# Second layer's input projection: the second 1024 weight rows in seven products too, beside attention

## The chip, the cores and the metric

The kernel runs on one core of one Trainium2 chip. The metric is the device time of one execution in microseconds (us).

## The reference, cut to what matters

Two sequences (512 and 256 tokens, 768 together, width 2048) go through two layers. The change lies in the second one:

```python
h = x @ odd_w_in[i]                       # [768, 2048] @ [2048, 8192]
q, k, v, g = jnp.split(h, 4, axis=-1)     # 16 heads of 128 each
y = (_dilated_mixture(q, k, v, pos) * jax.nn.silu(g)) @ odd_w_out[i]
x = _layernorm(DN_ALPHA * x + y, ln_g[layer], ln_b[layer])
```

`_dilated_mixture` turns the first 32 of each head's 128 features of q and k by position (rope), and is then attention within each sequence, with a fixed table added to the scores. Everything is float32. A product is made of three float32r matmuls: each factor is split in a high part (a cast, on ACT) and a low part (what is left, a subtraction on DVE or POOL), and high by high, high by low and low by high are summed.

## The kernel before

Activations lie feature-major: `xh` and `xl` hold 16 tiles of 128 features by 768 tokens. The projection of the second layer goes in two passes over the 2048 weight rows (the contraction).

**First pass, rows 0 to 1023** (class `Seven`, L664 to L778). Two blocks of 128 output features at a time (a *pair*, 32 pairs) are computed by Strassen's scheme: the weights of a pair are four tiles of 512 rows by 128 columns, the activations four quarters (512 features by 384 tokens), and seven products of 12 matmuls (128x384) take the place of eight. Sums and differences of the activation quarters are made once; those of the weights in `prep` (four subtractions and seven splits a pair, DVE L708 and L442, ACT L441); the sums of products in `product` (five additions out of PSUM on DVE, L738, and two copies on ACT, L740 and L742). `prep` is called three products ahead (`AHEAD = 3`), and the split weights have four buffers. The partial sums of each pair go to DRAM (`pd1`). `run` calls `each()` after every product, which takes one item off the list `c.q` of side work.

At the end of the pass the plain activations of rows 1024 to 2047 are restored from `z` by eight splits.

**Second pass, rows 1024 to 2047**, head by head for 16 heads: four blocks (q, k, v, gate), each of 48 matmuls 128x384 (`proj_f` with `k0=8`, L521), after which DVE adds the partial sum that was loaded from `pd1` some blocks before (`block`, L1293). q and k get rope on 32 partitions by 768 tokens and are split (`qk`, L1307 to L1310 and L442: shuffle, products with cos and sin, sum, cast on ACT, low part on POOL). Attention (class `Attn`) goes in steps of 128 queries, six steps a head: `scores`, two steps later `turn` (the probabilities transposed and split), three steps later `values` once a sequence is done. In `scores` DVE scales, adds the table and takes the maximum, negates it, ACT takes the exponential, DVE the reciprocal of the sum and the scaling of the probabilities (L827 to L832). The steps of a head are put into `c.q`, and run between the matmuls of later blocks:

```python
hd.qq = qk(block(h, 0), h % 2 * 2)
hd.kk = qk(block(h, 1), h % 2 * 2 + 1)
flush(c)
att.add(hd)
c.q += [nop] * (2 if h < 15 else 1) + [att.step] * (6 if h < 15 else att.left())
```

The output projection (`proj_t`, L565) follows; its activations are the heads' results, loaded back from `md` (`mix_in`) and split.

**What sets the order.** Each engine works off its queue in order and waits where an operand is late. The order in a queue is not simply that of the code: the framework plans the queues before the run, by its own expectation of durations, code order being the priority. DMAs are issued from SP, ACT or POOL; the issuing queue waits for the data that the DMA reads.

Of the kernel before, what the change touches and what calls it, by code (L numbers as in the profile page):

```python
# [665 lines left out]
class Seven:  # L666
# [11 lines left out]
    def __init__(self, c, ops, cols, dst, pool, outs):  # L678


        self.c, self.ops, self.cols, self.dst, self.pool, self.outs = c, ops, cols, dst, pool, outs
        self.raw, self.hl, self.acc, self.res = {}, {}, {}, {}

    def rows(self, n, b):
        w, f0, f1 = self.cols[n]
        return wf(w, b // 2, (f0, f1)[b % 2])
# [16 lines left out]
    def prep(self, n, i):  # L703
# [5 lines left out]
        new = lambda: self.pool.tile([128, 512], F32, tag="bt", name="bt", bufs=4)  # L709
# [12 lines left out]
    def product(self, n, i):  # L722
# [6 lines left out]
        xh, xl = self.ops[i]  # L729
# [35 lines left out]
    def run(self, seq, each):  # L765

        at = {}
        for m, (n, i) in enumerate(seq):
            at.setdefault(n, m)
        due = sorted(at.items(), key=lambda x: x[1])  # L770
        for m in range(-self.AHEAD, len(seq)):
            while due and due[0][1] <= m + self.AHEAD + 5:
                self.load(due.pop(0)[0])
            if m + self.AHEAD < len(seq):
                self.prep(*seq[m + self.AHEAD])
            if m >= 0:
                self.product(*seq[m])
                each()  # L778


class Attn:
# [5 lines left out]
    def __init__(self, c, pool, table=None, early=None):  # L787
        self.c, self.pool, self.table, self.early = c, pool, table, early or pool
        self.units, self.n = [], 0
# [9 lines left out]
    def step(self):  # L799
        u, n = self.units, self.n  # L800
        if n < len(u):
            self.scores(*u[n])
        if 0 <= n - 2 < len(u):
            self.turn(*u[n - 2])
        if 0 <= n - 3 < len(u) and u[n - 3][1] == u[n - 3][0].nt - 1:
            self.values(u[n - 3][0])
# [5 lines left out]
    def scores(self, seq, i):  # L812
# [13 lines left out]
        else:  # L826
            nc.vector.tensor_tensor_reduce(out=p, in0=s, in1=self.table[:, 384 - 128 * i:384 - 128 * i + nk],  # L827
                                           scale=1.0 / SQ128, scalar=-3e38, op0=ALU.add, op1=ALU.max, accum_out=st[:, 0:1])
# [3 lines left out]
        nc.vector.tensor_scalar(out=p, in0=p, scalar1=st[:, 2:3], scalar2=0.5, op0=ALU.mult, op1=ALU.mult)  # L832
# [4 lines left out]
    def turn(self, seq, i):  # L837
        c, nc, pool = self.c, self.c.nc, self.pool
        nt = seq.nt
        if i == 0:  # L840
            seq.pt = [pool.tile([128, nt, 128 * nt], F32R, tag=f"pt{x}{nt}", name=f"pt{x}{nt}") for x in "hl"]
# [4 lines left out]
        split_ps(nc, pv, *(t[:, :, 128 * i:128 * i + 128] for t in seq.pt))  # L846

    def values(self, seq):
        c, nc = self.c, self.c.nc
        nt = seq.nt  # L850
        o = ps_tile(c, "ps_o")[:, 0:128 * nt]
# [5 lines left out]
        seq.head.done(o, seq.t0, nt)  # L857
# [25 lines left out]
def hybrid_kernel(tc, x_p, x_s, w_in0, w_out0, a_re, a_im, log_dt, b_re, b_im, c_re, c_im, d_sk, glu_w, glu_b,  # L883
# [4 lines left out]
    with ExitStack() as es:  # L888
# [22 lines left out]
        pd1 = dr.tile([32, 128, 2, TOK], F32, name="pd1")  # L911
# [127 lines left out]
        with rpool("pk") as pk, ExitStack() as bes:  # L1039
# [89 lines left out]
            for k in range(8):  # L1129
# [5 lines left out]
        cols1 = ([(w1, 128 * h, 2048 + 128 * h) for h in range(16)] +  # L1135
                 [(w1, x + 256 * j, x + 256 * j + 128) for x in (4096, 6144) for j in range(8)])
        with rpool("po") as po:
# [90 lines left out]
            ops = half(0, 0), half(0, 3), half(8, 0), half(4, 0), half(8, 3), half(12, 0), half(4, 3)  # L1228
            n_first = 3
            with rpool("pw") as pw:  # L1230
                free, whole = [z[:, t, 0:768] for t in range(6)], {}

                def outs(n):
                    two = lambda f: [f[:, 0:HALF], f[:, HALF:768]]
                    if n < n_first:
                        return [pw.tile([128, HALF], F32, tag="early", name="early", bufs=2 * n_first) for _ in range(2)]
                    whole[n] = free.pop(0), free.pop(0)
                    free.extend(whole[n])
                    return two(whole[n][0]) + two(whole[n][1])

                def part_out(n, r):
                    if n < n_first:
                        for i in range(4):
                            store(c, pd1[n, :, i // 2, HALF * (i % 2):HALF * (i % 2) + HALF], r[i], 1)
                    else:
                        for i in range(2):
                            store(c, pd1[n, :, i], whole[n][i], 1)

                sv = Seven(c, ops, cols1, part_out, pw, outs)
# [10 lines left out]
                sv.run(sv.order(0, 32, n_first), lambda: fill(c))  # L1260
                flush(c)
                for k0, t0 in ((8, 0), (12, 3), (8, 3), (12, 0)):
                    for k in range(k0, k0 + 4, 2):
                        hi, lo = (a[:, k:k + 2, 128 * t0:128 * t0 + HALF].rearrange("p k (t n) -> p t k n", t=3) for a in (xh, xl))
                        raw = z[:, t0:t0 + 3, 128 * k:128 * k + 256].rearrange("p t (k n) -> p t k n", k=2)
                        split_sb(nc, raw, hi, lo, nc.vector)

        res0 = pool("res0", 1).tile([128, 6, 256], F32, name="res0")
# [9 lines left out]
        with rpool("pc") as pc:  # L1278
            cos1 = pc.tile([32, TOK], F32, name="cos1")
            sin1 = pc.tile([32, TOK], F32, name="sin1")  # L1280
            nc.sync.dma_start(cos1, c_rope1[0])
            nc.sync.dma_start(sin1, c_rope1[1])
            mixt = pc.tile([128, 896], F32, name="mixt")
            nc.sync.dma_start(mixt, c_mix)
            att = Attn(c, pc, mixt)

            def block(n, i):

                w, *f = cols1[n]
                t = raws.pop(0)  # L1290
# [3 lines left out]
                return t  # L1294

            raws, plan = [], []

            def fetch():

                if plan:  # L1300
                    n, i = plan.pop(0)
                    raws.append(pc.tile([128, TOK], F32, tag="raw", name="raw", bufs=4))
                    nc.sync.dma_start(raws[-1], pd1[n, :, i])

            def qk(t, k):
                sh = pc.tile([32, TOK], F32, tag="sh", name="sh", bufs=1)
                nc.vector.stream_shuffle(sh, t[0:32], SWAP)  # L1307
# [4 lines left out]
                return c.xh[k], c.xl[k]  # L1312

            def turn_v(t, i):

                vv = [a[4 + i].rearrange("p (t f) -> p t f", t=6) for a in (c.xh, c.xl)]

                def go():
                    for t0, n in SEQS:
                        ps = ps_tile(c, "ps_v")  # L1320
                        for j in range(n):
                            nc.tensor.transpose(ps[:, 128 * j:128 * j + 128], t[:, 128 * (t0 + j):128 * (t0 + j) + 128], c.ident)
                        split_ps(nc, ps[:, 0:128 * n].rearrange("p (j f) -> p j f", j=n), *(a[:, t0:t0 + n] for a in vv))

                return vv, go
# [5 lines left out]
            def mix_in(k):  # L1331
                if k < 15:
                    load_split(pc, md[k], c.xh[k], c.xl[k], 4, nc.vector, "raw")

            class Head1:
                def __init__(self, h):
                    self.h = h
# [7 lines left out]
                def v(self, t):  # L1345
                    return [a[:, t] for a in self.vv]

                def done(self, o, t0, nt):
                    if t0 == 0:
                        self.o = pc.tile([128, TOK], F32, tag="o1", name="o1", bufs=2)  # L1350
                    nc.scalar.copy(self.o[:, 128 * t0:128 * (t0 + nt)], o)
                    if t0:
                        self.finish()

                def finish(self):
                    nc.gpsimd.tensor_tensor(out=self.o, in0=self.o, in1=self.g, op=ALU.mult)
                    if self.h < 15:
                        store(c, md[self.h], self.o, 0)
                    else:
                        split_sb(nc, self.o, c.xh[15], c.xl[15])  # L1360

            for h in range(16):
                plan += [(h, 0), (h, 1), (16 + h // 2, h % 2), (24 + h // 2, h % 2)]
            fetch()
            fetch()
            for h in range(16):
                hd = Head1(h)
                fetch()
                hd.qq = qk(block(h, 0), h % 2 * 2)
                fetch()  # L1370
                hd.kk = qk(block(h, 1), h % 2 * 2 + 1)
                flush(c)
                att.add(hd)
                c.q += [nop] * (2 if h < 15 else 1) + [att.step] * (6 if h < 15 else att.left())
                fetch()
                hd.vv, go = turn_v(block(16 + h // 2, h % 2), h % 2)
                c.q.insert(0, go)
                fetch()
# [126 lines left out]
```

## Time and profile before

| | |
|---|---|
| runs | 2730.73, 2731.81, 2734.80 us (median 2731.81) |
| profiled execution | 2731.15 us, span 2729.3 us |
| PE (matmul) busy | 2613.1 us, 96% of the span |
| DVE, ACT, POOL busy | 1775.7, 903.7, 798.0 us |
| mean granted TensorE clock | 0.982 |
| first pass | about 1254 to 1741 us |
| second pass with attention | about 1741 to 2431 us |

PE is pipelined: a matmul's own duration (334 ns) is about twice the distance between two starts. For rates one reads distances and windows, not means.

### The profile page before, as it was taken

How to read it: one execution, taken by the hardware profiler on the slowest of the kernel's cores; microseconds unless marked ns; L12 is line 12 of the kernel's file. 1: busy time of each engine (PE TensorE's matmuls, PEld its weight loads, DVE VectorE, ACT ScalarE, POOL GpSimd, SP SyncE). 2: the span in 40 equal slices, each digit the busy share in tenths (PEclk: the TensorE clock that was granted, in tenths of full speed). 3: DMA queues.
4: the chain of work that ended last, by engine and by line, in shares of the span. 5: the costliest groups of instructions: out<-in, count | busy, mean ns of one | idle time of the engine just before them, and what ended most of it. 6: DMA issues, size and time to landing. Idle time of an engine off the chain costs nothing.

```text
span 2729.3 us, 41667 instructions
## 1 busy us (share of the span) xinstructions
PE 2613.1 (96%) x15824; PEld 2493.2 (91%) x15824; DVE 1775.7 (65%) x3504; ACT 903.7 (33%) x1775; POOL 798.0 (29%) x554
## 2 busy tenths in 40 slices
PE   8899999998998999998999999999999999999997
PEld 7899999998997898887999999999999999998886
DVE  6578888858357842238766666577767677773527
ACT  4222222222235521116433333334333333341111
POOL 2645555536554430002000000222212122234404
PEclk9999999999999999998999999999999999999998
DMA  5333333332434362225344434333332333345222
GB/s 149 114 91 93 98 92 93 90 80 75 128 109 136 121 219 74 66 82 178 122 126 132 125 123 135 116 97 101 93 97 87 98 101 95 106 136 183 76 69 112
DMA packets 349769, 301.56 MB, mean 110 GB/s; under 512 B 57665, under 2 KB 298561, under 8 KB 348673
## 3 DMA queue, kind: packets, MB, share of 16 engines
q1 hardware_dynamic: 337712, 287.13, 34.5%
q0 software_dynamic: 2496, 8.39, 1.1%
q10 hardware_dynamic: 9360, 3.38, 0.8%
q8 instruction: 125, 2.05, 0.3%
q14 instruction: 76, 0.61, 0.1%
HBM read 231.38 MB, written 67.44 MB: 109 GB/s over the span
## 4 chain that ended last, share of the span: by engine, by line
PE 75%; DVE 12%; DMA 4%; issue 3%; POOL 2%; SPq 2%; ACT 2%; DVEq 0%; ACTq 0%; POOLq 0%
PE pt L565 22%; PE pa L521 13%; PE pb L521 13%; PE ps_y L733 7%; PE ps_z L733 5%; PE ps_x L733 5%; PE ps_o L856 3%; PE ps_sc L820 3%; PE ps_pt L844 2%; DVE tmpv L227 1%; DMA wr<-in_even_w_in_dram 1%; SPq L351 1%; PE ps_y L410 1%; DVE ca L229 1%; DVE win L229 1%
## 5 line engine op out<-in xcount | busy, mean ns | idle before, releaser
L441 ACT CAST wh<-wr 128x512 fp32r<-128x512 f32 x442 | 273.9, 623 | 895.9 <-PE pt L565 334.1
L442 DVE TENSOR_TENSOR wl<-wr,wh 128x512 fp32r<-128x512 f32 x274 | 241.4, 884 | 359.6 <-ACT wh L441 359.5
L565 PE MATMUL pt<-wh,xh 128*128 128x256 f32 (+1 forms) x1392 | 458.4, 330 | 7.8 <-ACT wh L441 6.8
L565 PE MATMUL pt<-wl,xh 128*128 128x256 f32 (+1 forms) x1392 | 457.0, 328 | 1.5 <-POOL wl L442 1.3
L565 PE MATMUL pt<-wh,xl 128*128 128x256 f32 (+1 forms) x1392 | 456.1, 328 | 0.0
L521 PE MATMUL pa<-xh,wh 128*128 128x384 f32 x960 | 337.7, 352 | 21.4 <-ACT wh L441 18.1
L442 POOL TENSOR_TENSOR wl<-wr,wh 128x512 fp32r<-128x512 f32 x168 | 232.9, 1397 | 354.9 <-ACT wh L441 313.0
L521 PE MATMUL pa<-xh,wl 128*128 128x384 f32 x960 | 326.3, 340 | 9.8 <-POOL wl L442 9.6
L521 PE MATMUL pa<-xl,wh 128*128 128x384 f32 x960 | 325.7, 339 | 0.0
L521 PE MATMUL pb<-xl,wh 128*128 128x384 f32 x960 | 325.3, 339 | 0.0
L521 PE MATMUL pb<-xh,wl 128*128 128x384 f32 x960 | 325.1, 339 | 0.0
L521 PE MATMUL pb<-xh,wh 128*128 128x384 f32 x960 | 325.0, 339 | 0.0
L565 PEld LDWEIGHTS pt<-wh,xh 128*128 128x128 f32 x1392 | 265.6, 191 | 32.6 <-ACT wh L441 7.7
L565 PEld LDWEIGHTS pt<-wl,xh 128*128 128x128 f32 x1392 | 266.2, 191 | 24.6 <-POOL wl L442 1.8
L565 PEld LDWEIGHTS pt<-wh,xl 128*128 128x128 f32 x1392 | 266.1, 191 | 22.4
L521 PEld LDWEIGHTS pa<-xh,wh 128*128 128x128 f32 x960 | 182.8, 191 | 26.1 <-ACT wh L441 20.2
L521 PEld LDWEIGHTS pa<-xh,wl 128*128 128x128 f32 x960 | 182.9, 191 | 13.1 <-POOL wl L442 13.1
L521 PEld LDWEIGHTS pb<-xh,wh 128*128 128x128 f32 x960 | 183.4, 191 | 1.5
L521 PEld LDWEIGHTS pa<-xl,wh 128*128 128x128 f32 x960 | 183.1, 191 | 0.0
L521 PEld LDWEIGHTS pb<-xl,wh 128*128 128x128 f32 x960 | 183.1, 191 | 0.0
L521 PEld LDWEIGHTS pb<-xh,wl 128*128 128x128 f32 x960 | 182.7, 190 | 0.0
L1275 POOL DMA_DIRECT2D lrow<-in_ln_g_dram x8 | 4.5, 563 | 477.8 <-DMA wr<-in_odd_w_in_dram 475.8
(350 smaller groups left out, 5569.6 us busy)
## 6 DMA issues: line engine op xcount, KB each, us to landing
wr<-in_even_w_in_dram SPq DMA_DIRECT2D x144, 256.0 KB, 3.2
wr<-in_odd_w_in_dram SPq DMA_DIRECT2D x134, 256.0 KB, 2.9
b<-in_odd_w_in_dram SPq DMA_DIRECT2D x128, 256.0 KB, 2.9
raw<-pd SPq DMA_DIRECT2D x64, 384.0 KB, 3.4
pd<-z SPq DMA_DIRECT2D x58, 384.0 KB, 2.5
wr<-in_even_w_out_dram SPq DMA_DIRECT2D x64, 256.0 KB, 2.7
wr<-in_odd_w_out_dram SPq DMA_DIRECT2D x64, 256.0 KB, 2.8
nd<-z POOLq DMA_DIRECT2D x12, 512.0 KB, 4.3
```

Source lines behind the costliest of these rows:

```text
L227: e.tensor_tensor(out=tmp, in0=pt(9 + j), in1=xt(sx), op=ALU.mult)
L229: e.tensor_tensor(out=out, in0=out, in1=tmp, op=op)
L351: nc.sync.dma_start(s.m[16 * st_:16 * st_ + 16], s.kd[:, :, 16 * st_:16 * st_ + 128].rearrange("g c x -> c g x"))
L410: nc.tensor.matmul(o, s.ca[:, 0, g, 1:9].rearrange("p j c -> p (j c)"), s.xs[:, 0:8, :, g].rearrange("p j r -> p r j"), start=False, stop= ...
L441: nc.scalar.copy(hi, src)
L442: (eng or nc.gpsimd).tensor_tensor(out=lo, in0=src, in1=hi.bitcast(F32), op=ALU.subtract)
L521: nc.tensor.matmul(out[n][s][:, 0:HALF], wt[:, j], xt[k][:, HALF * s:HALF * s + HALF], start=k == k0 and i == 0, stop=k == nk - 1 and i == 2)
L565: nc.tensor.matmul(view[t], xt[k][:, tok], wt[:, j], start=first and i == 0 and ti % per == 0, stop=last and i == 2 and ends)
L733: nc.tensor.matmul(ps, w[:, k], x(k), start=i < 3 and k == j == 0, stop=k == 3 and j == 2, skip_group_check=i >= 3)
L820: nc.tensor.matmul(s, a[:, qs], b[:, ks], start=j == 0, stop=j == 2)
L844: nc.tensor.transpose(ps[:, 128 * j:128 * j + 128], seq.ps[i][:, 128 * j:128 * j + 128], c.ident)
L856: nc.tensor.matmul(o, a, b[:, j], start=j == 0 and x == 0, stop=j == nt - 1 and x == 2)
```

## The change

The second pass is done by `Seven` as well. `ops` and `cols` are indexed so that pairs 32 to 63 are the same columns with weight rows 1024 to 2047. The pairs are ordered by two heads at a time: (q,k) of head 2j, v of both heads, (q,k) of head 2j+1, gates of both. One list of products runs through both passes (`run` becomes a generator). The activation sums for the second pass are made on DVE during the first (`next_parts`), and their splits are written over the first pass's quarters as these have had their last use.

After the seventh product of a pair `ready1` runs: a DMA from POOL's queue adds the 768 KB partial sum from `pd1` into the result tile (768 KB, three buffers). For q and k, rope copies the 32 leading rows of four 384-token pieces by four POOL DMAs to a tile of 128 partitions, does shuffle, two products and a sum there (all DVE), and copies back by four POOL DMAs; then both blocks are split (low parts on DVE). The head's six attention steps are queued behind five empty items. In `Attn`, the maximum comes out negated (the negation goes), ACT scales the probabilities in place of DVE, and `values` runs for two query blocks at a time.

```diff
+            ops = [ops + (half(4, 3),), ops + (half(12, 3),)]
...
+            seq = sv.order(0, 32, n_first)
+            products = sv.run(seq + sv.order(32, 64, 32), lambda: fill(c))
...
+                def next_parts(t):
+                    split_sb(nc, k4(a22), xh[:, 12:16, tok], xl[:, 12:16, tok], nc.vector)
+                    tt(a22, a21, a22, ALU.add)
+                    tt(a21, a11, a21, ALU.subtract)
+                    tt(sb[:, u, 0:512], a22, a11, ALU.subtract)
+                    tt(sb[:, u, 512:1024], a12, sb[:, u, 0:512], ALU.subtract)
+                c.q += [nop] * 14 + sum(([lambda t=t: next_parts(t)] + [nop] * 9 for t in range(3, 6)), [])
...
-                ps = proj_f(c, [(w, f[i])], 16, k0=8)[0]
-                for p, sl in halves(ps):
-                    nc.vector.tensor_tensor(out=t[:, sl], in0=p, in1=t[:, sl], op=ALU.add)
...
-                nc.gpsimd.tensor_tensor(out=sh, in0=sh, in1=sin1, op=ALU.mult)
-                nc.vector.tensor_tensor(out=t[0:32], in0=t[0:32], in1=cos1, op=ALU.mult)
-                nc.vector.tensor_tensor(out=t[0:32], in0=t[0:32], in1=sh, op=ALU.add)
-                split_sb(nc, t, c.xh[k], c.xl[k])
...
+            def place1(n):
+                t = pc.tile([128, 4, HALF], F32, tag="res", name="res", bufs=3)
+            def ready1(n, r):
+                nc.gpsimd.dma_start(flat, pd1[n], accum_op=ALU.add)
+                if kind in (0, 2):
+                    flush(c)
+                    hd = hds[2 * j + kind // 2]
+                    rope(t)
+                    hd.qq, hd.kk = parts(blocks[0], "q"), parts(blocks[1], "k")
+                    att.add(hd)
+                    s = att.step
+                    if n < 30:
+                        c.q += [nop] * 5 + [s, nop, s, nop, s, nop, s, s, s]
+                    else:
+                        c.q += [nop] * 4 + [s] * att.left()
+                elif kind == 1:
+                    c.q[3:3] = [lambda i=i: turn_v(blocks[i], hds[2 * j + i]) for i in range(2)]
+                else:
+                    for i in range(2):
+                        hd = hds[2 * j + i]
+                        gate_sb(blocks[i], hd.g)
+                        hd.finish()
+            def rope(t):
+                rt, sh = (pc.tile([128, HALF], F32, tag=a, name=a, bufs=1) for a in ("rt", "sh"))
+                for i in range(4):
+                    nc.gpsimd.dma_start(rt[32 * i:32 * i + 32], t[0:32, i])
+                nc.vector.stream_shuffle(sh, rt, SWAP)
+                nc.vector.tensor_tensor(out=rt, in0=rt, in1=cos4, op=ALU.mult)
+                nc.vector.tensor_tensor(out=sh, in0=sh, in1=sin4, op=ALU.mult)
+                nc.vector.tensor_tensor(out=rt, in0=rt, in1=sh, op=ALU.add)
+                for i in range(4):
+                    nc.gpsimd.dma_start(t[0:32, i], rt[32 * i:32 * i + 32])
...
-            nc.vector.tensor_scalar(out=st[:, 0:1], in0=st[:, 0:1], scalar1=-1.0, scalar2=None, op0=ALU.mult)
-            nc.scalar.activation(out=p, in_=p, func=AF.Exp, bias=st[:, 0:1], scale=1.0, accum_out=st[:, 1:2])
+            nc.scalar.activation(out=p, in_=p, func=AF.Exp, bias=st[:, 0:1], scale=-1.0, accum_out=st[:, 1:2])
...
+            nc.scalar.activation(out=p, in_=p, func=AF.Copy, scale=st[:, 2:3])
...
-            order1 = [6, 7, 8, 9, 10, 11, 12, 13, 0, 1, 2, 3, 4, 5, 14, 15]
+            order1 = [0, 1, 2, 3, 8, 9, 10, 11, 12, 13, 4, 5, 6, 7, 14, 15]
```

`mix_in` now takes its raw tiles from the same three buffers as the results, and no head is loaded back before the last product. The space of `Seven`'s weight tiles is freed only after the last product, and `res0` (first block of the residual, with its two multiplications on POOL) is placed there.

## Rows read from the trace of the kernel before

**Rows 1.** The page, parts 1 and 5: engine busy time; POOL's issue of one DMA.

```profile
PE 2613.1 (96%) x15824; PEld 2493.2 (91%) x15824; DVE 1775.7 (65%) x3504; ACT 903.7 (33%) x1775; POOL 798.0 (29%) x554
...
L1275 POOL DMA_DIRECT2D lrow<-in_ln_g_dram x8 | 4.5, 563 | 477.8 <-DMA wr<-in_odd_w_in_dram 475.8
```

**Rows 2.** Windows: length, busy of PE, PEld, DVE, ACT, POOL, clock, DMA, GB/s.

```profile
1595.21:1624.33 29.12, 29.12 (x170) 29.12 (x169) 19.55 (x33) 10.25 (x19) 0.00 (x0) 1.00 0.43 135
...
1740.00:1775.00 35.00, 29.94 (x173) 29.62 (x171) 15.90 (x25) 5.38 (x9) 14.44 (x8) 0.99 0.52 158
...
1864.97:1908.26 43.29, 43.29 (x255) 41.99 (x255) 31.21 (x64) 16.36 (x33) 10.08 (x5) 1.00 0.32 95
...
2410.00:2462.00 52.00, 49.25 (x323) 46.64 (x322) 35.39 (x72) 27.18 (x53) 15.91 (x11) 0.97 0.45 143
```

**Rows 3.** Chain of waits in time order: start, length, engine, work; first pass.

```profile
1301.93 2.08 PE ps_y L733 x12
```

**Rows 4.** DVE's groups by line, 1864.97 to 1908.26 us (one head, second pass).

```profile
L442 DVE TENSOR_TENSOR wl<-wr,wh 128x512 fp32r<-128x512 f32 x8 | 7.0, 876 | 6.8 <-ACT wh L441 6.8
L1309 DVE TENSOR_TENSOR raw<-raw,cos 32x768 f32<-32x768 f32 x2 | 4.2, 2124 | 0.0
...
L1293 DVE TENSOR_TENSOR raw<-pa,raw 128x384 f32<-128x384 f32 x4 | 2.2, 551 | 3.9 <-PE pa L521 3.9
L1293 DVE TENSOR_TENSOR raw<-pb,raw 128x384 f32<-128x384 f32 x4 | 2.2, 545 | 0.0
L1307 DVE STREAM_SHUFFLE sh<-raw 32x768 f32<-32x768 f32 x2 | 2.0, 1023 | 0.0
L832 DVE TENSOR_SCALAR pp<-pp,sst 128x512 f32<-128x512 f32 x4 | 2.0, 510 | 0.1
L1310 DVE TENSOR_TENSOR raw<-raw,sh 32x768 f32<-32x768 f32 x2 | 1.9, 938 | 0.0
L832 DVE TENSOR_SCALAR pp<-pp,sst 128x256 f32<-128x256 f32 x2 | 1.9, 928 | 0.0
```

**Rows 5.** Groups by line of the whole run: casts, splits, sums, subtractions.

```profile
L442 DVE TENSOR_TENSOR wl<-b,wh 128x512 fp32r<-128x512 f32 x122 | 84.4, 692 | 32.8 <-ACT wh L441 32.6
...
L441 ACT CAST wh<-b 128x512 fp32r<-128x512 f32 x122 | 76.1, 623 | 171.8 <-PE ps_z L733 81.6 <-PE ps_y L733 46.5 <-PE ps_x L733 42.2
...
L738 DVE TENSOR_TENSOR z<-ps_y,z 128x384 f32<-128x384 f32 x90 | 50.0, 556 | 52.5 <-PE ps_y L733 52.5
...
L708 DVE TENSOR_TENSOR wr<-b,b 128x512 f32<-128x512 f32 x32 | 22.1, 692 | 30.5 <-DMA b<-in_odd_w_in_dram 30.5
...
L442 DVE TENSOR_TENSOR xl<-raw,xh 128x768 fp32r<-128x768 f32 x15 | 14.9, 991 | 15.6 <-ACT xh L441 15.5
```

**Rows 6.** Waits of engines on loads: total us, times, longest.

```profile
DVE wr L708 <- DMA b<-in_odd_w_in_dram: 30.5, 29, 2.1
...
ACT xh L441 <- DMA raw<-md: 14.0, 9, 2.7
```

**Rows 7.** DMA issues: count, KB each, median us from issue to landing.

```profile
z<-nd SPq DMA_DIRECT2D x7, 768.0 KB, 10.7
...
lrow<-in_ln_g_dram POOLq DMA_DIRECT2D x8, 128.0 KB, 3.7
...
res<-nd SPq DMA_DIRECT2D x1, 768.0 KB, 5.4
```

**Rows 8.** Timeline of DVE: start, length, line, work, idle before.

```profile
1838.75 2.25 DVE L442 TENSOR_TENSOR wl<-wr,wh 128x512 fp32r<-128x512 f32 x1
...
1841.33 0.94 DVE L1310 TENSOR_TENSOR raw<-raw,sh 32x768 f32<-32x768 f32 x1
...
1845.73 0.54 DVE L1293 TENSOR_TENSOR raw<-pb,raw 128x384 f32<-128x384 f32 x1
```

**Rows 9.** Timeline of POOL: the low part of that head's K block.

```profile
1852.86 2.02 POOL L442 TENSOR_TENSOR xl<-raw,xh 128x768 fp32r<-128x768 f32 x1 [3.29 <-ACT xh L441]
```

**Rows 10.** Timeline of PE: that head's first scores.

```profile
1863.89 0.39 PE L820 MATMUL ps_sc<-xh 128*128 128x512 f32 x1
```

More of the change, by code (lines that the diff above doesn't have):

```diff
@@ L802, in step @@
             self.scores(*u[n])
+        if self.pairs and 0 <= n - 3 < len(u) and u[n - 3][1] % 2:
+            self.values(*u[n - 3])
         if 0 <= n - 2 < len(u):
             self.turn(*u[n - 2])
-        if 0 <= n - 3 < len(u) and u[n - 3][1] == u[n - 3][0].nt - 1:
-            self.values(u[n - 3][0])
+        if not self.pairs and 0 <= n - 3 < len(u) and u[n - 3][1] == u[n - 3][0].nt - 1:
+            self.values(*u[n - 3])
         self.n += 1
@@ L856, in values @@
                 nc.tensor.matmul(o, a, b[:, j], start=j == 0 and x == 0, stop=j == nt - 1 and x == 2)
-        seq.head.done(o, seq.t0, nt)
+        seq.head.done(o, seq.t0 + i + 1 - nq, nq)
 BLOCKS = ((0, 256), (256, 512), (768, 512), (1280, 512), (1792, 256))
@@ L1227, in hybrid_kernel @@
             half = lambda k0, t0: tuple(lambda k, x=x: x[:, k0 + k, 128 * t0:128 * t0 + HALF] for x in (xh, xl))
-            ops = half(0, 0), half(0, 3), half(8, 0), half(4, 0), half(8, 3), half(12, 0), half(4, 3)
+            ops = half(0, 0), half(0, 3), half(8, 0), half(4, 0), half(8, 3), half(12, 0)
+            ops = [ops + (half(4, 3),), ops + (half(12, 3),)]
             n_first = 3
[L1230 to L1249, printed above, removed]
@@ new lines, in hybrid_kernel, with outs @@
+            wes = es.enter_context(ExitStack())
+            pw = wes.enter_context(tc.tile_pool(name="pw", bufs=1))
+            free, whole = [z[:, t, 0:768] for t in range(6)], {}
+            places = []
+            def outs(n):
+                two = lambda f: [f[:, 0:HALF], f[:, HALF:768]]
+                if n >= 32:
+                    return places[0](n)
+                if n < n_first:
+                    return [early.tile([128, HALF], F32, tag="early", name="early", bufs=2 * n_first) for _ in range(2)]
+                whole[n] = free.pop(0), free.pop(0)
+                free.extend(whole[n])
+                return two(whole[n][0]) + two(whole[n][1])
@@ L1259, in hybrid_kernel @@
                 c.q += late + [rest]
-                sv.run(sv.order(0, 32, n_first), lambda: fill(c))
+                for m in range(seq.index((n_first - 1, 6)) + 1):
+                    next(products)
                 flush(c)
[L1262 to L1266, printed above, removed]
@@ L1314, in turn_v @@
[L1314 to L1325, printed above, removed]
+            cos4, sin4, mixt = (pc.tile([128, n], F32, name=a) for a, n in (("cos4", HALF), ("sin4", HALF), ("mixt", 896)))
@@ L1359, in finish @@
                     else:
[L1360 to L1378, printed above, removed]
-                t = block(24 + h // 2, h % 2)
-                hd.g = pc.tile([128, TOK], F32, tag="g1", name="g1", bufs=2)
-                gate_sb(t, hd.g)
-                if h in (12, 13):
-                    mix_in(h - 6)
+                        split_sb(nc, self.o, c.xh[15], c.xl[15], nc.vector)
+            hds = [Head1(h) for h in range(16)]
+            places += [place1, ready1]
+            for _ in products:
+                pass
+            wes.close()
+            res0 = pool("res0", 1).tile([128, 6, 256], F32, name="res0")
             c.weng = nc.gpsimd
```

148 lines of the change are left out of this document (101 added, 47 removed).

## The prediction

> **What bounds the kernel now.** I read the page first, to see which engine is the full one: PE is busy for 96% of the span [rows 1]. That share is an average, so I then cut windows out of the two passes. In the first pass, one window of 29.12 us (two pairs of blocks) shows PE busy for all of it and DVE for 19.55 [rows 2]; in the second, one head takes 43.29 us, PE busy for all of it, DVE for 31.21 and ACT for 16.36. The chain of waits gives the step of a product in the first pass: 12 matmuls of 384 columns in 2.08 us, 0.1733 us each [rows 3]. So both passes run at PE's pace at the full clock (1.00 in both windows, the 2.4 GHz level), and a matmul less is 0.1733 us less, as long as nothing else comes late. In a head, 4 x 48 such matmuls are 33.28 us, and attention on PE is what is left, 43.29 - 33.28 = 10.0 us.
>
> Then I looked for where the second pass isn't full: 5.06 us of PE's time are lost in the 35 us around the change of passes, and 2.75 us in the 52 us in which attention ends and the output projection begins [rows 2]. There is no other gap to win.
>
> Last I looked at what the change puts in danger, the way from a head's projected K block to its first scores. In one head, DVE adds the partial sum to K until 1846.27 [rows 8], the low part of K is done at 1854.88 [rows 9], and the first scores run at 1863.89 [rows 10]. The way takes 8.6 us and has 9.0 us to spare.
>
> **The change, part by part.** *Matmuls.* Before, 64 blocks of 48 are 3072; after, 32 pairs of 7 x 12 are 2688. 384 x 0.1733 = 66.6 us less, 4.16 a head; a head's period at PE's pace falls from 43.29 to 39.1 us. All of it is on the path that sets the end. Attention keeps its columns (the same values in halves of 256 columns), so its 10.0 us stay.
>
> *DVE.* Per head, out go eight splits (7.0 us), four additions of two halves (2.2 + 2.2), rope on 32 lanes (2.0 + 4.2 + 1.9) and the scaling (2.0 + 1.9): 23.4 us [rows 4]. In come 14 splits and eight subtractions at 0.69 (15.2), ten additions at 0.556 (5.6), two low parts of 768 columns at 0.99 that POOL did before (2.0) [rows 5], and rope on 128 lanes: half the columns of the shuffle (0.5) and three products or sums at three quarters of a 512-column one (0.52), 2.1 us, an estimate from [rows 4, 5]. That makes 24.9, and DVE has about 31.2 + 1.5 = 32.7 us of work in 39.1. The splits of the second pass took 0.876 instead of 0.69, one of them 2.25 beside a multiplication on POOL [rows 4, 8]; at that size 14 of them cost 2.6 more. So 33 to 35 us: DVE hides under PE with 4 to 6 us to spare, where it had 12.
>
> *ACT.* 16.4 plus six more casts, four copies out of PSUM and six scalings, each taken at the cast's 0.62 [rows 5]: 16 x 0.62 = 9.9, so 26 of 39.1. Hidden. *POOL* loses both sin products and low parts, and issues eight rope DMAs and two adding ones a head at 0.56 each [rows 1]; 5.6 us. Hidden, but POOL's queue now holds waits: the rope copies wait there for the adding DMA, the copies back for DVE, and behind them stand the next pair's adding DMA and the head's multiplication with its gate, whose store SP waits for. All of these have the 14 products of a head (29 us) to come.
>
> *The new way from projection to scores.* After a pair's seventh product: one DVE addition, 0.56 [rows 5]. Then the adding DMA of 768 KB. No row shows an accumulating DMA; the nearest are plain loads of that size, 5.4 us alone and 10.7 among others [rows 7]. It has to read its target as well, so I take 8, in the middle, with both ends kept. Then four small copies issued 0.56 apart, the last landing 3.7 after its issue (POOL's 128 KB load, the nearest row; these are 48 KB): 5.4. DVE's rope 2.1. Four copies back, 5.4. Cast 0.84 or less, low parts of q and k 2.0. Together 24 us (21.7 to 27), against the 8.6 of before [rows 1, 5, 7]. The Trainium skill (DMA: Bandwidth & Descriptors, section on the anatomy of one DMA on the gpsimd path) gives such a DMA 2.0 us plus its bytes at 436 GB/s. For 128 KB that is 2.3, and the row shows 3.7, so the trace does not agree; by the page the way would be about 17 us, an estimate.
>
> In the code the scores stand only five products (10.4 us) behind. If the queues kept the order of the code, PE would wait some 13.5 us in each head. But they don't: DVE runs a later block's split (1838.75) ahead of the sum that ends rope (1841.33), though the code has it behind [rows 8]. The queue order is planned by expected durations, so later products will stand ahead of the scores, and what PE waits for is only how much later the way is than the plan. The trace has a measure of that for a DMA: DVE waits in the first pass 30.5 us in 29 times for the weights, 1.05 each, and ACT 14.0 in 9 times, 1.56, for the heads' results [rows 6]. In the new way two engines that feed PE stand before such a landing, DVE before the shuffle and ACT before the cast of q. I take 1.05 twice, 2.1 us a head, 33.6 in all, between 0 (planned too long) and 13.5 (not planned at all). Three products of prepared weights (6.2 us) lie between a waiting DVE and PE, so the waits of DVE and ACT cost nothing besides the scores. The gates' wait on ACT and that of v's transposes on PE, each behind one DMA of 8 us, have three products or more to cover it; at no cover, 1 us each for eight pairs of heads, 16 us.
>
> *Ends.* The sums for the second pass (12 subtractions and three splits, 15 x 0.69 = 10 us) fall into a pass in which DVE is idle for 9.6 of 29.1 us: nothing. Around the change of passes the same pipeline runs on; of the 5.06 us lost there I count 4 won. At the end, 2.75 us were lost; now the heads come back from DRAM only after the last product and share buffers with it, and POOL multiplies the residual in the same stretch as it splits output weights: 0 to 10 us more, which I leave at 0.
>
> **The sum.** The profiled execution took 2731.15, 0.66 below the median. 2731.81 - 66.6 + 33.6 - 4 = 2694.8, so 2695.
>
> **Rivals.** *A: everything hides.* The plan allows for the DMAs, PE waits for under 1 us a head: 2661 to 2677. For it: in the second pass PE waited for nothing over the whole head [rows 2]. Against: the loads of [rows 6] were late by a microsecond although they are simple.
>
> *B: slower.* One mechanism, the first scores of each head waiting for q and k, whose way now goes three times through DRAM or POOL's DMAs. From 4.16 us a head on, the saving is gone (with the 4 us of the boundary, 4.4). If the adding DMA alone takes 10.7 where the plan has a plain 5.4, and the rope groups come 1.05 late each, the wait is 7.4 us: 2731.8 - 70.6 + 118 = 2780. For it: 24 us against 10.4 in the code, no row for such a DMA. Against: a whole head's period, 39 us, is there to move the scores in.
>
> *C: DVE becomes the bound.* Its 33 to 35 us have 4 to 6 to spare; it loses them if its waits behind DMAs, twice a head and with the gate, pass that. At 7 us of waiting the period is 41 to 42, and the time 2731.8 - 4 - 16 x (43.3 - 41.5) = 2699, within the forecast's range but with another engine full. Waits of 1.05 speak against it.
>
> *D: no change,* B at its turning point, 2726 to 2737.
>
> **How the numbers follow.** A measurement here tells about 0.2% (5.5 us) from no change. Forecast with 1 to 3.5 us of wait a head, C included: 0.53 (2677 to 2717). A: 0.18. A wait of 3.5 to 4 us: 0.02. D: 0.06. B beyond: 0.21. Faster 0.73, same 0.06, slower 0.21. The range starts at A's low end, 2662, and goes up to a wait of 5.7 us a head, 2731.8 - 70.6 + 91 = 2752, which leaves out some 0.15 of B and little of A. The forecast's own range is 2677 to 2717.
>
> **What would show it.** Matmuls of the second pass: 2688 at the line of `product`, and two heads between 78 and 84 us. Busy DVE 66 to 70 of them. Waits before the scores of a head: 2 us if right, none for A, over 4.4 for B, with DVE's shuffle or ACT's cast of q waiting for a DMA before them. The adding DMA between 5.4 and 10.7. The prediction is wrong if that DMA is far slower, if the queues keep the scores where the code has them, or if the end of attention loses more than 10 us.

## The result and the profile after

The changed kernel takes 2833.77 us in the median (2831.25 to 2836.59, 4 runs), against 2731.27 for the kernel before in the same runs: a ratio of 1.0376, 95% interval 1.0357 to 1.0395. The forecast was 2695 (2662 to 2752): wrong side, and outside the range. The profiled execution has a span of 2834.8 us, 105.5 longer than before's.

The page of the changed kernel, part 1 (before's line is in [rows 1]):

```profile
PE 2604.0 (92%) x15632; PEld 2475.1 (87%) x15632; DVE 1817.6 (64%) x3572; ACT 1038.5 (37%) x2054; POOL 757.2 (27%) x649
```

192 matmul records fewer than before, not 384, since values now run in halves; but busy PE falls by 9.1 us alone, and what isn't busy rises from 116.2 to 230.8. DVE has 64% on average. To find the place I cut both traces at 1741 us, where the first pass has just ended, and at the end of the last matmul of the input projection. Windows of the kernel before (length, busy of PE, PEld, DVE, ACT, POOL, granted clock, DMA share, GB/s):

```profile
1741.00:2430.78 689.78, 684.58 (x4004) 664.77 (x4004) 489.70 (x980) 257.50 (x513) 168.69 (x85) 1.00 0.34 101
2430.78:2729.30 298.52, 276.72 (x1501) 240.00 (x1499) 149.65 (x239) 58.87 (x98) 102.01 (x54) 0.97 0.35 116
```

and of the changed one:

```profile
1741.00:2525.07 784.07, 668.29 (x3783) 640.09 (x3782) 513.79 (x1027) 380.20 (x769) 122.79 (x177) 0.91 0.39 93
2525.07:2834.80 309.73, 282.34 (x1531) 246.10 (x1530) 149.87 (x239) 67.60 (x115) 110.08 (x58) 0.96 0.38 121
```

The first pass takes as long as before. The second pass is 94.3 us longer, the rest 11.2. In the second pass PE was idle for 5.2 us and is now for 115.8, 7.2 a head. And its granted clock was 1.00 and is 0.91: PE spends part of this pass at the 1.2 GHz level. That is most of why 16.3 us of busy time went and not the 66.6 of the matmuls left out; e6 below shows the share.

What PE waits for in the second pass of the changed kernel (engine, line, what waits, on what: total, times, longest):

```profile
PE ps_sc L825 <- ACT kh L441: 64.8, 14, 7.5
PE ps_y L734 <- DVE res L739: 38.3, 16, 4.5
PE ps_sc L825 <- issue: 7.9, 1, 7.9
PE ps_o L870 <- DVE ptl L447: 3.4, 4, 1.1
```

Two waits, then: the scores for the first part of the split k, and a product's first matmul for the sum by which DVE empties that PSUM bank. One head shows both. Its timeline, POOL first (start, length, engine, line, work, count, idle time before and what ended it):

```profile
2054.73 0.90 POOL L1346 DMA_DIRECT2D res<-pd  x1 [13.83 <-DVE res L739]
2062.17 2.03 POOL L1373 DMA_DIRECT2D rt<-res  x4 [6.55 <-DMA res<-pd]
2069.93 1.97 POOL L1379 DMA_DIRECT2D res<-rt  x4 [5.72 <-DVE rt L1377]
```

DVE in the same head:

```profile
2062.88 0.69 DVE L709 TENSOR_TENSOR wr<-b,b 128x512 f32<-128x512 f32 x1 [3.93 <-DMA b<-in_odd_w_in_dram]
...
2065.54 0.55 DVE L739 TENSOR_TENSOR res<-ps_y,res 128x384 f32<-128x384 f32 x1
...
2066.62 0.58 DVE L1374 STREAM_SHUFFLE sh<-rt 128x384 f32<-128x384 f32 x1
...
2069.09 0.55 DVE L1377 TENSOR_TENSOR rt<-rt,sh 128x384 f32<-128x384 f32 x1
...
2074.62 0.96 DVE L442 TENSOR_TENSOR ql<-res,qh 128x768 fp32r<-128x768 f32 x1 [3.31 <-DMA res<-rt]
```

ACT's two casts, for which the scores wait:

```profile
2073.76 0.83 ACT L441 CAST qh<-res 128x768 fp32r<-128x768 f32 x1 [4.69 <-DMA res<-rt]
2074.98 0.83 ACT L441 CAST kh<-res 128x768 fp32r<-128x768 f32 x1 [0.39 <-DMA res<-rt]
```

and PE:

```profile
2066.24 0.41 PE L734 MATMUL ps_y<-xh,wh 128*128 128x384 f32 x1 [2.25 <-DVE res L739]
...
2075.86 0.80 PE L825 MATMUL ps_sc<-kh,qh 128*128 128x512 f32 x1 [7.27 <-ACT kh L441]
2076.46 0.41 PE L870 MATMUL ps_o<-pth,xh 128*128 128x256 f32 x1
2076.86 0.80 PE L825 MATMUL ps_sc<-kl,qh 128*128 128x512 f32 x1
```

From the issue of the adding DMA to the scores it is 21.1 us: 7.4 for that DMA, 4.5 until the shuffle starts, 3.3 of rope, 5.0 until the last copy back has landed, for which k's cast waits, and 0.9 for that cast. In PE's queue six products stand between the pair's seventh and the scores (five that the code puts there and one more), 12.5 us, of which 11.6 lie behind that issue. The rest, 9.5 us, PE stands idle, in two parts: 2.25 and 7.27. In the trace it is six products in all 16 heads. Every second head waits like this one, 7.6 to 11.0 us from the issue on; in the others 26 attention matmuls of the head before stand between as well, and PE waits 3.7 to 7.6. After the wait the first scores, 512 columns, take 0.80; at the full clock such matmuls take 0.39 [rows 10]: this is the lower level.

The first part has a cause of its own. DVE had stood 3.93 us before the weights of the next pair, and the sum that PE wanted was queued behind. DMA issues between 2050 and 2064 us (KB each, median us from issue to landing):

```profile
b<-in_odd_w_in_dram SPq DMA_DIRECT2D x3, 256.0 KB, 4.5
res<-pd POOLq DMA_DIRECT2D x1, 768.0 KB, 7.2
```

The row of these loads over the whole run:

```profile
b<-in_odd_w_in_dram SPq DMA_DIRECT2D x256, 256.0 KB, 2.9
```

Of the three in the window, one had landed just after the adding DMA was issued; the two beside it took 5.9 and 4.5. The Trainium skill (DMA: Bandwidth & Descriptors, section on issuing engines not being separate DMA queues) says that DMAs issued from different engines run on the same 16 DMA engines; the trace agrees, 4.5 against 2.9 for loads from SP's queue beside a transfer from POOL's. Over the second pass, the 24 loads issued while an adding DMA ran took 4.4 in the median, the 60 with none beside them 2.8. In eight of the 16 cases the sum stood behind such a wait alone, in the other eight behind the shuffle's wait for the last of rope's copies (2.2 to 2.7 us, once 6.5), mostly with a shorter wait for weights before it.

### The profile page after: what moved, and what is told of

The parts are those of the page before. It is cut to its first block, busy times and chain, and to the rows that moved or that the text cites. A ratio compares the mean times of both kernels' runs of the same rounds, so it can differ in the third digit from the quotient of the medians.

```text
span 2834.8 us, 41853 instructions
## 1 busy us (share of the span) xinstructions
PE 2604.0 (92%) x15632; PEld 2475.1 (87%) x15632; DVE 1817.6 (64%) x3572; ACT 1038.5 (37%) x2054; POOL 757.2 (27%) x649
## 5 line engine op out<-in xcount | busy, mean ns | idle before, releaser
L734 PE MATMUL ps_y<-xh,wh 128*128 128x384 f32 x768 | 268.0, 349 | 39.4 <-DVE res L739 38.3
L734 PE MATMUL ps_y<-xh,wl 128*128 128x384 f32 x768 | 262.7, 342 | 0.0
L734 PE MATMUL ps_y<-xl,wh 128*128 128x384 f32 x768 | 262.1, 341 | 0.0
L442 DVE TENSOR_TENSOR wl<-b,wh 128x512 fp32r<-128x512 f32 x250 | 177.8, 714 | 35.6 <-ACT wh L441 35.1
L734 PE MATMUL ps_x<-xh,wh 128*128 128x384 f32 x512 | 180.6, 353 | 2.6 <-ACT early L741 1.6
L734 PE MATMUL ps_x<-xh,wl 128*128 128x384 f32 x512 | 174.5, 341 | 8.3 <-DVE wl L442 8.3
L521 PE MATMUL pa<-xh,wh 128*128 128x384 f32 x448 | 160.6, 359 | 21.4 <-ACT wh L441 18.1
L734 PE MATMUL ps_x<-xl,wh 128*128 128x384 f32 x512 | 175.0, 342 | 0.0
L734 PE MATMUL ps_z<-xh,wh 128*128 128x384 f32 x512 | 172.9, 338 | 0.0
L734 PE MATMUL ps_z<-xh,wl 128*128 128x384 f32 x512 | 171.3, 335 | 0.0
```

Source lines behind the costliest of these rows:

```text
L442: (eng or nc.gpsimd).tensor_tensor(out=lo, in0=src, in1=hi.bitcast(F32), op=ALU.subtract)
L521: nc.tensor.matmul(out[n][s][:, 0:HALF], wt[:, j], xt[k][:, HALF * s:HALF * s + HALF], start=k == k0 and i == 0, stop=k == nk - 1 and i == 2)
L734: nc.tensor.matmul(ps, w[:, k], x(k), start=i < 3 and k == j == 0, stop=k == 3 and j == 2, skip_group_check=i >= 3)
```

## The experiments

Theory 1: the way from a pair's seventh product to the split q and k is longer than the products queued before the scores; PE waits for the difference, and loses clock by waiting. Theory 2, the rival: with 14 splits more on DVE and 32 transfers of 768 KB more, an engine or the DMA engines are full, and waits move wherever something is late. The table has all runs, with PE's busy and idle time and the granted clock from 1741 us to the last product; each column is of the profiled execution, but for the median and the ratio to the kernel before (95% interval). In e2, e8 and e9 some 45 matmuls (8 us) of the first pass still lie behind 1741 us.

| kernel | median us | ratio | second pass | PE busy | PE idle | clock |
|---|---|---|---|---|---|---|
| before | 2731 | | 689.8 | 684.6 | 5.2 | 1.00 |
| after | 2833.8 | 1.0376 [1.0357, 1.0395] | 784.1 | 668.3 | 115.8 | 0.91 |
| e1 scores later | 2782.8 | 1.0179 [1.0162, 1.0197] | 728.0 | 652.0 | 76.0 | 0.96 |
| e2 rope by copies | 2773.2 | 1.0140 [1.0115, 1.0165] | 729.6 | 660.2 | 69.4 | 0.96 |
| e3 early load of q, k | 2727.0 | 0.9981 [0.9971, 0.9991] | 680.8 | 643.1 | 37.7 | 0.98 |
| e4 no rope | 2723.6 | 0.9971 [0.9960, 0.9983] | 669.2 | 636.5 | 32.7 | 0.98 |
| e5 no adding DMA | 2688.2 | 0.9843 [0.9824, 0.9862] | 647.0 | 629.1 | 17.9 | 1.00 |
| e6 = e2 + e3 | 2696.3 | 0.9867 [0.9846, 0.9887] | 644.4 | 630.1 | 14.3 | 1.00 |
| e8 = e6, DVE splits at the end | 2694.8 | 0.9870 [0.9849, 0.9890] | 651.5 | 637.7 | 13.8 | 1.00 |
| e9 = e8, two heads a buffer | 2696.8 | 0.9884 [0.9864, 0.9904] | 651.9 | 636.6 | 15.3 | 1.00 |
| e10 plain DMA | 2790.4 | 1.0218 [1.0198, 1.0239] | 742.1 | 654.0 | 88.1 | 0.93 |
| e11 = e1 + e3 | 2750.4 | 1.0073 [1.0049, 1.0098] | 701.7 | 648.6 | 53.1 | 0.96 |

**e1: the attention steps three products later.**

```diff
-                        c.q += [nop] * 5 + [s, nop, s, nop, s, nop, s, s, s]
+                        c.q += [nop] * 8 + [s] * 6
...
-                    c.q[3:3] = [lambda i=i: turn_v(blocks[i], hds[2 * j + i]) for i in range(2)]
+                    c.q[4:4] = [lambda i=i: turn_v(blocks[i], hds[2 * j + i]) for i in range(2)]
```

> Only the places of a head's six attention steps change: eight empty items and six steps in a row in place of five empty ones with gaps (the two transposes of v one place later). Theory 1, the way from the seventh product to split q and k (some 21 us) is longer than the work that stands ahead of the first scores: three products more are 6.2 us, so PE's wait for the cast of k falls from some 4.5 us a head to 1 or less, the wait behind DVE's shuffle stays; 2755 to 2790 us. Theory 2, an engine or the DMAs are too full beside attention: moving the steps frees nothing, 2825 to 2845 us.

51 us less than the changed kernel, without an operation or a byte less. Eight products and in every second head eight and two thirds stand before the scores now (six for the last head, which the edit leaves alone), and the wait for k's first part falls from 64.8 to 36.0, 2.2 a head where 1 or less was expected. In the head shown above PE waits 9.5 us with six products between; in the same head of e1 it waits 3.9 with eight and two thirds (5.6 us more work), and the way from the seventh product stays at 22 us. The waits at products were expected to stay; they fall from 38.3 to 6.2. New waits appear before the values, since the six steps run one product apart. PE's waits in e1's second pass:

```profile
PE ps_sc L825 <- ACT kh L441: 36.0, 14, 5.1
PE ps_o L870 <- DVE ptl L447: 11.2, 11, 1.3
PE ps_o L870 <- ACT pth L446: 10.0, 6, 2.2
...
PE ps_y L734 <- DVE res L739: 6.2, 4, 4.3
```

**e2: rope's eight small DMAs replaced.** ACT copies the four pieces to 32 partitions each, and DVE's last sum writes straight back, in four parts.

```diff
-                    nc.gpsimd.dma_start(rt[32 * i:32 * i + 32], t[0:32, i])
+                    nc.scalar.copy(rt[32 * i:32 * i + 32], t[0:32, i])
...
-                nc.vector.tensor_tensor(out=rt, in0=rt, in1=sh, op=ALU.add)
                 for i in range(4):
-                    nc.gpsimd.dma_start(t[0:32, i], rt[32 * i:32 * i + 32])
+                    p = slice(32 * i, 32 * i + 32)
+                    nc.vector.tensor_tensor(out=t[0:32, i], in0=rt[p], in1=sh[p], op=ALU.add)
```

> Rope's eight small DMAs a head become four copies on ACT across partitions, and the final sum is written by DVE straight back (four sums of 32x384); the adding DMA stays. Theory 1: the way gets shorter by some 8 us (two groups of four DMAs at 4.5 to 5 us each, against 3 us of ACT and DVE work), so it is about 13 us against 10.4 to 12.5 of work ahead; PE's waits for k and behind the shuffle nearly vanish, 2710 to 2750 us. Theory 2: ACT and DVE get more work, time as the changed kernel or above, 2830 to 2860.

61 us less, but 23 above the top of what was expected. The scores wait little (8.1 us for k's first part, 7.1 for its second); the wait for the adding DMA has moved to ACT and DVE, whose queues also carry the sums and casts that feed PE. Waits in e2's second pass, of PE, DVE and ACT:

```profile
PE ps_y L734 <- DVE res L739: 24.5, 8, 4.1
PE ps_o L870 <- DVE ptl L447: 13.9, 7, 2.5
PE ps_z L734 <- DVE res L739: 13.0, 7, 3.3
PE ps_sc L825 <- ACT kh L441: 8.1, 10, 2.8
PE ps_sc L825 <- DVE kl L442: 7.1, 7, 1.1
```

```profile
DVE sh L1374 <- ACT rt L1373: 36.8, 8, 6.0
```

```profile
ACT rt L1373 <- DMA res<-pd: 50.8, 16, 4.4
```

**e3: the adding DMA taken out of the way, for q and k.** Before the pair's first product SP loads the partial sum into the result tile, and DVE adds each product to it (those lines, in `product`, are left out below); v and gates keep the adding DMA, rope its eight DMAs.

```diff
...
+                if n % 2 == 0:
+                    nc.sync.dma_start(t.rearrange("p a n -> p (a n)"), pd1[n - 32])
+                    sv.base[n] = pc.tile([128, HALF], F32, tag="rt", name="rt", bufs=1)
...
-                nc.gpsimd.dma_start(flat, pd1[n], accum_op=ALU.add)
+                if n % 2:
+                    nc.gpsimd.dma_start(flat, pd1[n], accum_op=ALU.add)
```

> For q and k the partial sum is loaded by SP into the result tile before the pair's first product, and DVE adds onto it (four more DVE sums a pair, one ACT copy less); v and gates keep the adding DMA, rope keeps its eight DMAs. Theory 1: the way is shorter by the adding DMA, 7 us, and PE's waits fall as in the run with rope on ACT: 2715 to 2760 us. Theory 2: DVE has 2 us more a head, time as the changed kernel or above. If the adding DMA alone were to blame, this would win everything and the run with rope on ACT nothing.

107 us less than the changed kernel, although DVE has more to add (535.2 us busy in the second pass against 513.8). So a fuller DVE isn't what holds it. PE's waits in e3's second pass:

```profile
PE ps_sc L839 <- ACT kh L441: 14.1, 12, 2.6
PE ps_o L884 <- DVE ptl L447: 9.2, 8, 1.3
```

**e6: the edits of e2 and e3 together.**

> Both shortenings together: partial sum of q and k loaded ahead, rope by ACT copies. Theory 1: the way is 6 to 7 us, below the 10.4 us of five products; PE has no wait left at the scores, the clock in the second pass is back at 1.00, two heads take 78 to 80 us in place of 98.7, and only the end of attention still loses: 2670 to 2700 us. Theory 2: 2800 or more. A rival on the clock (it fell for another reason than the waits): the waits go, but the granted clock stays near 0.90 and the time near 2740.

137 us less than the changed kernel, and 1.3% faster than the one before: with e8 and e9 the only version of the whole computation here that gains over 1%. PE no longer waits for k, and for sums 1.7 us in all; the largest of its waits is now this one:

```profile
PE ps_o L884 <- ACT pth L446: 5.5, 7, 1.9
```

With the waits gone, the granted clock is back at 1.00, on the same matmuls and beside a fuller DVE, which answers the rival on the clock. A stretch of 100 us of its second pass (columns as in the windows above):

```profile
2000.00:2100.00 100.00, 98.60 (x601) 95.84 (x601) 87.20 (x182) 63.32 (x129) 6.01 (x4) 1.00 0.37 102
```

DVE is at 87% here, against 66% over the changed kernel's second pass, and PE at 99%. Theory 2 in the form "DVE is too full" is out. The operations that stand in for the eight DMAs, in e6, by ACT and by DVE (groups by line: busy us, mean ns):

```profile
L1391 ACT COPY rt<-res 32x384 f32<-32x384 f32 x49 | 25.1, 511 | 14.6 <-DVE res L739 12.9
```

```profile
L1397 DVE TENSOR_TENSOR res<-rt,sh 32x384 f32<-32x384 f32 x52 | 28.3, 544 | 0.8
```

Four of each, 4.2 us a head, and they stay in the engines; the two groups of DMAs took 8.3 in the head above, from first issue to last landing (3.3 and 5.0).

**e4 and e5: each part left out alone.**

```diff
-                    rope(t)
```

> The changed kernel without its call of rope: q and k are not rotated, so the eight 48 KB transfers, the shuffle and the three 128x384 operations of DVE are left out of each head; the adding DMA stays. The rope of the first kernel's second layer has no other place, so this leaves out part of the computation. Theory 1 (the way from the seventh product to the scores is longer than the products queued between): the way of one head falls from 21 us to about 9.5 (adding DMA 7.5 and the first part of the split 1.7), which is under the 12.5 us of products queued ahead; DVE no longer stands behind rope's first transfer, so the wait of PE for sums of DVE goes too. About 2700 to 2730, and the wait of PE for the first split of k under 15 us in all. Theory 2 (engines or transfers too full): only DVE's 1.6 us per head go, 2790 to 2830.

```diff
-                nc.gpsimd.dma_start(flat, pd1[n], accum_op=ALU.add)
```

> The changed kernel without the adding DMA for q, k, v and gates: the first 1024 weight rows' part is missing in all four (it is still computed and stored, not read again); rope's transfers stay. Theory 1: the way falls from 21 us to about 13.5, near the 12.5 us queued ahead: the wait of PE for the first split of k falls from 67 us to about 15, as with the partial sums loaded early, and the time is that run's or some microseconds less, 2715 to 2730. If the adding DMA cost mainly through its bytes (25 MB in all) rather than by its place in the way, leaving it out would be worth clearly more than loading early was: under 2700.

Both leave out a part of the computation. e4 lands where theory 1 put it, 110 us less. e5 is 27 us below its lower bound, in the branch that I had set for a cost beyond the place in the way. With no 768 KB transfer in the second pass (DMA share 0.26, against 0.39), DVE waits 11.2 us for weights, against 42.2 in the changed kernel up to the same time; e3, which still has 32 such transfers, 25.4.

**e10: the same DMA without adding.**

```diff
-                nc.gpsimd.dma_start(flat, pd1[n], accum_op=ALU.add)
+                nc.gpsimd.dma_start(flat, pd1[n])
```

> The changed kernel with the DMA from POOL's queue as a plain load in place of an adding one: the first 1024 rows' partial sum overwrites the second's, so the sum of both, a part of the computation, is left out; bytes written, place in the queue and waits are the same. If the adding itself makes that DMA slow (6.9 us for 768 KB against 4.7 for the early load from SP's queue), it takes some 5 us here, the way falls by 2 and the time by some 30 us, to 2795 to 2810. If what costs is that any 768 KB transfer stands in the way and beside the weights' loads, the time stays within 10 us of the changed kernel's: 2824 to 2840.

43 us less, a little more than the first branch said: adding itself has a price. The two rows of DMA issues, of the changed kernel and of e10:

```profile
res<-pd POOLq DMA_DIRECT2D x32, 768.0 KB, 6.9
```

```profile
res<-pd POOLq DMA_DIRECT2D x32, 768.0 KB, 4.8
```

PE's waits in e10 show what the two kinds of wait have to do with each other:

```profile
PE ps_sc L825 <- ACT kh L441: 74.0, 14, 7.8
PE ps_sc L825 <- issue: 7.5, 1, 7.5
PE ps_y L734 <- DVE res L739: 5.2, 5, 1.8
```

The wait before products is all but gone (38.3 to 5.2), that before scores has grown (64.8 to 74.0): PE, less held up, comes to the scores sooner and waits there. Together it waits 5.5 us a head, not 7.2; 1.7 less, for a DMA 2.1 shorter. So the sum of both waits follows the length of the way, as theory 1 has it, and most of the 38.3 us is no loss of its own: without it PE would have waited at the scores.

**e11: the early load with the later steps**, the edits of e3 and e1.

> q and k loaded early as before, rope's eight transfers left as they are, and the attention steps three products later in the list. Theory 1: the way without the adding DMA is about 13.5 us, and the products queued ahead of the scores grow to eight or more, 16.6 us: the scores wait for next to nothing, and the second pass goes near PE's pace: 2690 to 2708, though rope's transfers all stay. If rope's transfers cost by their traffic or by the space that they take in POOL's and DVE's queues, the time stays near that of the early load alone, 2718 to 2730.

A miss for theory 1: 2750, 23 us slower than e3. It is right about the scores, which wait for k no longer, but the time goes to another wait. PE's waits in e11's second pass, then one place of DVE's timeline:

```profile
PE ps_o L884 <- DVE ptl L447: 35.4, 13, 4.1
PE ps_o L884 <- ACT pth L446: 12.1, 7, 2.3
...
PE ps_sc L839 <- DVE kl L442: 0.8, 1, 0.8
```

```profile
2050.42 0.69 DVE L709 TENSOR_TENSOR wr<-b,b 128x512 f32<-128x512 f32 x1 [5.08 <-DMA b<-in_odd_w_in_dram]
...
2053.18 0.42 DVE L447 TENSOR_TENSOR ptl<-ps_pt,pth 128x256 fp32r<-128x256 f32 x1
```

PE stands from 2049.63 to 2053.65 for that last operation, and DVE's queue stood 5.08 us before weights, whose last load was issued at 2042.69 and took 7.6 us. Beside it ran not an early load but the adding DMA of a v or gate pair, which e3 and e11 keep (8.1 us; its issue is the first row below). The DMA engines were busy for 0.94 of the 4 us from 2044 on:

```profile
2041.55 0.94 POOL L1364 DMA_DIRECT2D res<-pd  x1 [8.51 <-DVE res L739]
```

```profile
2044.00:2048.00 4.00, 4.00 (x25) 3.82 (x24) 0.59 (x2) 2.57 (x6) 0.00 (x0) 1.00 0.94 199
```

This is the rule in e11: of the 59 us that DVE waits for weights in its second pass, 52 are for loads that ran beside an adding DMA. The edit also put the steps closer together, so that a late split of probabilities has one product to cover it instead of two; which of the two weighs more wasn't tried. What theory 2 keeps is this: an adding DMA of 768 KB beside a pair's four weight loads makes these late, and DVE, in order, makes everything behind them late. Why e6, with the same transfers of 768 KB as e3, waits only 12.7 us for weights is open.

**e8 and e9: the end of attention.** e6 still loses 7.7 us behind the last product (306.2 us against 298.5), not the 16 that the text of e8 has. e8 splits the first output block's weights on DVE, e9 packs two loaded heads to a buffer as well.

```diff
-            c.weng = nc.gpsimd
+            c.weng = nc.vector
...
-                    raw = pc.tile([128, 4, HALF], F32, tag="res", name="res", bufs=3).rearrange("p a n -> p (a n)")[:, 0:TOK]
+                    if not packs:
+                        f = pc.tile([128, 4, HALF], F32, tag="res", name="res", bufs=3).rearrange("p a n -> p (a n)")
+                        packs.extend([f[:, 0:TOK], f[:, TOK:2 * TOK]])
+                    raw = packs.pop(0)
```

> The version with q and k loaded early and rope by copies, with one change behind attention: in the first output block the lower parts of the weights are split by DVE (0.71 us each) in place of POOL (1.53 us each). SP, which issues the loads, stood 23.6 us behind POOL's splits there. If these waits carry the 16 us that the end of attention still loses against the first kernel, 2680 to 2690; if the loads of the mixed heads through three buffers carry it, 2694 to 2700, no change.

> The run before with a second change: the heads of the output projection are loaded two to a buffer, so that six places and not three stand before the split. If the buffers carry the loss, 5 to 10 us less than the run before: 2675 to 2688. If the DMA engines themselves are the limit in these 46 us (their share is 0.68 there), no change against the run before.

Neither moves the time (2694.8 and 2696.8); the end takes 304.1 and 309.4. Neither POOL's splits nor the buffers carry that loss. e6's trace shows where it lies: behind the last product PE waits 11.3 us in all, against 3.8 in the kernel before, and most of it is one wait, for the last head's probabilities:

```profile
2404.11 0.58 PE L884 MATMUL ps_o<-pth,xh 128*128 128x256 f32 x1 [7.65 <-ACT pth L446]
```

ACT casts these late: its queue, in order, had stood twice before that for heads that come back from DRAM:

```profile
2395.88 0.83 ACT L441 CAST xh<-res 128x768 fp32r<-128x768 f32 x1 [3.88 <-DMA res<-md]
...
2400.58 0.83 ACT L441 CAST xh<-res 128x768 fp32r<-128x768 f32 x1 [3.24 <-DMA res<-md]
...
2403.50 0.56 ACT L446 CAST pth<-ps_pt 128x512 fp32r<-128x512 f32 x1
```

No run put attention's casts ahead of these, so what that would win isn't shown. (The share of the DMA engines in the first 46 us is 0.60 in e6 and e8, not 0.68 as e9's text has it.)

## Why the prediction was wrong

Measured against its sum, from the two profiled spans: forecast -37.0 (matmuls -66.6, waits +33.6, change of passes -4), measured +105.5. The 142.5 between are 81.0 of PE's idle time in the second pass (+110.6 in place of +29.6), 50.3 of its busy time there (-16.3 in place of -66.6) and 11.2 at the end.

**The step that failed** is in the way from projection to scores: "The queue order is planned by expected durations, so later products will stand ahead of the scores, and what PE waits for is only how much later the way is than the plan." The plan moved one product, no more; six stand before the scores, five of them put there by the code. The one row that I had taken as evidence was a split run 2.6 us ahead of a sum; it said nothing of a move by 10 us. So PE waits for all of the way that the products between don't cover, 21.1 - 11.6 = 9.5 us in the head shown, and not for a landing's lateness of 2.1: 7.2 us a head in the mean. The text had computed the other end, 13.5 with no planning at all, and named this condition among those that would make it wrong; it should have been the centre. e1 confirms the step from the other side: only the order changed, and 51 us came back.

**The way itself** was sized rightly: counted as in the forecast, from the sum behind the seventh product, it is 22.2 us in the head shown, against 24 (21.7 to 27). The adding DMA takes 6.9 (8 taken, 5.4 to 10.7), rope's groups of four 3.4 and 4.5 in the median (5.4 each); what DVE's queue adds before and within rope was not in the forecast.

**That "the waits of DVE and ACT cost nothing besides the scores"** was wrong too. Prepared weights cover late splits, but not the sums that empty PSUM banks, which stand in the same queue behind a late DMA: 38.3 us at products here, 37.5 in e2, and the splits of probabilities in e11. By e10 most of those of the changed kernel would have been lost at the scores otherwise.

**The clock** had no price in the sum. The changed kernel and e6 issue the same matmuls, and the changed kernel's take 668.3 us in the second pass and e6's 630.1: 38 us, at granted clocks of 0.91 and 1.00. Through all versions the clock falls as PE's idle time rises. With these 38 us rival B, which had priced a wait of 7.4 at 2780, would have been near the result. Its mechanism, the scores waiting for q and k, is what happened, at a chance of 0.21; its size was right by luck, since it came from an adding DMA of 10.7 us against a plan of 5.4, and that DMA took 6.9.

**What held, and what held in part.** The matmuls left out: in e6, at clock 1.00, PE's busy time per head is 39.4 us, against 39.1 forecast. Against the kernel before, though, that is 54.4 us less and not 66.6: the average head there was busy for 42.8 us, not for the 43.29 of the one that the forecast read, and this makes 8 of the 12 us between. DVE hides: 513.8 of 784 us, and even at 87% (e6) PE stays full, so C is out. The end: the "0 to 10 us" left at 0 were 11.2, half of it PE's busy time, in e6 still 7.7, all of it waiting.

## What to carry to other kernels

When a change lengthens the way between two steps, count how many instructions stand between them in the queue of the engine that waits, and take those as the cover; that a planner will find more has to be seen in a row that moves as far. A DMA in such a way costs its place first: load a partial sum before the products and add it on an engine, and move 32 rows between partitions by an engine's copy. Its bytes cost as well where other loads run beside it, as e5 and e11 show. Add what the clock costs to any forecast of waits on TensorE.

## What was not expected of the hardware

- An adding DMA of 768 KB from POOL's queue takes 6.9 us in the median, the same without adding 4.8, a plain load from SP's queue in e3 4.7.
- Loads of 256 KB from another queue, issued while it runs, take 4.4 us in the median, with none beside them 2.8; issued while a plain one of that size runs, 3.3 in e10 and 4.1 in e3.
- ACT copies 32x384 to other partitions in 0.51 us, and DVE adds 32x384 with its output in other partitions in 0.54; 48 KB by DMA takes 1.8 to 2.2 from issue to landing in the changed kernel (3.2 back in e11), and 0.5 on the queue that issues it.
- After PE had stood for 7.27 us, the scores that take 0.39 us for 512 columns at the full clock took 0.80, the 1.2 GHz level; over a pass that is idle for 15% the granted clock was 0.91, for 5 to 6% 0.98, for 2% 1.00.
